# A residual tile held in SBUF, norm sums moved to TensorE, rstd by ln and exp, and a TensorE without waits on itself

## The chip, the cores and the metric

The kernel runs as one program on the eight NeuronCores of one Trainium2 chip, one batch element per core. The metric is the device time of the slowest core in microseconds (us). Cores 0 to 3 form die 0, cores 4 to 7 die 1. In some executions the cores of one die, or of both, are granted a lower TensorE clock and run some per cent longer (the changed kernel's own: 11180.00 us with mean clocks of 0.825 to 0.827 on die 1 and 0.877 on die 0, where its fast runs take 9956.56 to 9958.34 us at 0.950 to 0.959); such an execution is called slow here, whatever the kernel, and is never compared with a fast one. A second measure is used: the mean span of the four cores of an *undisturbed die*, meaning one whose mean granted clock was 0.95 or more, taken as the median over all such dies of a kernel's runs. Fast runs mostly have mean clocks of 0.95 to 0.96 on both dies.

## The reference

Two layers over 2048 latent tokens (and a 256-token context in front of the first mixer), each a macaron: SwiGLU feed-forward, token mixer, SwiGLU feed-forward. Layer 0 mixes with a bidirectional RG-LRU, layer 1 with a Fourier transform. Every sub-layer is wrapped in two RMS norms, so each reads and writes the residual stream `x`.

```python
def rmsnorm(x, g):
    y = x * lax.rsqrt(jnp.mean(x * x, axis=-1, keepdims=True) + EPS)
    return y * g

def ffn_sublayer(x, g_pre, g_post, shift, scale, gate, w_in, w_out):
    y = swiglu(modulate(rmsnorm(x, g_pre), shift, scale), w_in, w_out)
    return x + MACARON * gate * rmsnorm(y, g_post)

# one layer (D_MODEL 2048, D_FF 5632, fp32 in and out)
x = ffn_sublayer(x, g[0], g[1], sh1, sc1, gt1, ffn_w_in[i, 0], ffn_w_out[i, 0])
...                                              # context the same way, in layer 0
hx = modulate(rmsnorm(x, g[2]), sh2, sc2)
y = rglru_mixer(hx, hc, ...) if is_rec else fourier_mixer(hx, ...)
x = x + gt2 * rmsnorm(y, g[3])
x = ffn_sublayer(x, g[4], g[5], sh3, sc3, gt3, ffn_w_in[i, 1], ffn_w_out[i, 1])

# inside rglru_mixer, for each direction and for each of 16 channel groups
r = sigmoid(block_diag(v, wa, ba)); i = sigmoid(block_diag(v, wx, bx))
a = exp(-RG_C * r * softplus(-lam)); b = sqrt(-expm1(2 * log(a))) * i * v
h_t = a_t * h_{t-1} + b_t                        # linear scan
out = (gelu(g_lat) * (h_forward + h_backward)) @ w_out
```

## The kernel before

Operations are recorded with the tiles that they read and write, and waits are derived from that. Each engine counts its finished operations in a semaphore of its own (`E_pe`, `E_act`, ...). An operation that writes a tile waits for the tile's last writer, also where the last writer was the same engine:

```python
    def _wait(self, stream, ev):
        if ev is None:
            return
        key, val = ev
        if self.seen[stream].get(key, 0) >= val:
            return
        self.seen[stream][key] = val
        self.eng[stream].wait_ge(self.sems[key], val)
```

This reaches TensorE (PE) in the feed-forward output phases, where one PSUM pair (two sums of 128x512 fp32 side by side, `sbank(k, 0, n)` and `sbank(k, 1, n)`) is filled by two operations, one per half of the hidden width. The second waits until the first is finished, not just issued:

```python
            for (a, b) in parts:                 # [(0, 22), (22, 44)]
                ...                              # load this half's weights
                def pe(e, ...):
                    for h in range(2):
                        for c in range(a, b):
                            ins = e.matmul(sbank(k, h, n), buf[...], rhs(c, h), start=(c == 0), stop=(c == nk - 1))
                S.op("pe", pe, reads=[rb] + r_rhs, writes=spair_res(k))
```

The reciprocal root of a norm (`rstd`) takes ScalarE (ACT) and VectorE (DVE):

```python
        S.op("act", lambda e: e.activation(out=a3, in_=spair(k, n), func=AF.Sqrt, bias=epsb[:], scale=1.0 / D), ...)
        S.op("dve", lambda e: e.reciprocal(out=acc[:, :2 * n], in_=acc[:, :2 * n]), ...)
```

The RG-LRU loop issues, for each of 16 channel groups, the gates of this channel among the projection groups of the next one (`take`):

```python
            take(vch, 6)                         # six projection groups of the next channel
            for q in gq[0]:                      # gates, direction 0, each followed by one group
                q(); take(vch)
            pmul(c, 0)
            ...
            for q in gq[1]:
                q(); take(vch)
            pmul(c, 1)
            ...
            expo(c, 0); ...; expo(c, 1)          # exponentials, then the rest of the projections
            ...
            for d in range(2):
                msqrt(d); scan(d)
```

The *output map* `@ w_out` works on two tiles of 1024 tokens. Each of 16 steps makes one 128-row block of `y`, copies it to a ring buffer, stores it to HBM, squares it and adds the square to an accumulator on DVE. While tile 1 is computed, tile 0 is post-normed, added to `x` and pre-normed for its feed-forward, in half-blocks: `post_steps` loads `y` and `x` and stores `x`, and `pre_steps` loads `x` once more.

```python
        def mix_y(i, steps):
            acc, r_acc = accs[1 - i], r_accs[1 - i]
            it = Inter(steps, KC - 1)
            for m in range(KC):
                it.tick()                        # some post/pre steps of the other tile
                k = next_slot(); mix_mm(m, i, k, range(KC))        # (first three steps are cut here)
                load_wm(i * KC + m + 4)
                for h in range(2):
                    eb, re, dn = ev.next()       # ring of three buffers
                    S.op("act", ... func=AF.Copy ...)
                    S.dma("sp", dn + "y", ... out=ys[...], in_=eb[:] ...)
                    acc_add(acc, r_acc, 512, h, m == 0, sbank(k, h, 512), [rPS[2 * k + h]])
            it.flush()
        mix_y(0, None)
        mix_y(1, post_steps(tiles[0], 1, 0, 0, 1) + pre_steps(tiles[0], 0, 0, 2, W.dst, W.r_dst))
```

Of the kernel before, what the change touches and what calls it, by code (L numbers as in the profile page):

```python
# [8 lines left out]
F32 = mybir.dt.float32  # L9
BF16 = mybir.dt.bfloat16  # L10
AF = mybir.ActivationFunctionType
ALU = mybir.AluOpType
# [24 lines left out]
class Sched:  # L37
# [51 lines left out]
    def _wait(self, stream, ev):  # L89
        if ev is None:  # L90
            return
        key, val = ev
        if self.seen[stream].get(key, 0) >= val:
            return
        self.seen[stream][key] = val
        self.eng[stream].wait_ge(self.sems[key], val)
# [84 lines left out]
def build(nsub=6):  # L181
# [63 lines left out]
    def spair(k, n):  # L245
        return PS[:, k * 1024:(k + 1) * 1024].rearrange("p (h x) -> p h x", h=2)[:, :, :n]
# [47 lines left out]
    def modcol(l, q, kc, which):  # L294
        i = (q * 16 + kc) * 2 + which
        return mods[l][:, i:i + 1]
# [9 lines left out]
    def dercol(l, s, which, kind, kc):  # L306
        i = ((l * 3 + s) * 2 + which) * 32 + kind * 16 + kc
        return der[:, i:i + 1]
# [77 lines left out]
    def rstd(acc, r_acc, n, k=None, slot=None):  # L386
        if k is None:
            k = next_slot() if slot is None else slot

            def pe(e):  # L390
                ins = None
                for h in range(2):
                    ins = e.matmul(sbank(k, h, n), ones[:], acc[:, h * n:(h + 1) * n], start=True, stop=True)  # L393
                return ins
            S.op("pe", pe, reads=[r_acc, r_const], writes=spair_res(k))
        a3 = acc[:, :2 * n].rearrange("p (h x) -> p h x", h=2)
        S.op("act", lambda e: e.activation(out=a3, in_=spair(k, n), func=AF.Sqrt, bias=epsb[:], scale=1.0 / D),
             reads=spair_res(k) + [r_const], writes=[r_acc])
        S.op("dve", lambda e: e.reciprocal(out=acc[:, :2 * n], in_=acc[:, :2 * n]), reads=[r_acc], writes=[r_acc])

    def acc_add(acc, r_acc, n, h, first, src, r_src):
        a = acc[:, h * n:(h + 1) * n]
# [225 lines left out]
    def merged_segs(tl):  # L628
        out = []
        for h in range(2):  # L630
            for (off, w, src, dst, t0, which) in tl.halves[h]:
                off += h * tl.n
                p = out[-1] if out else None
                if p and p[0] + p[1] == off and p[2] is src and p[4] + p[1] == t0 and p[5] == which:
                    out[-1] = (p[0], p[1] + w) + p[2:]
                else:
                    out.append((off, w, src, dst, t0, which))
        return out

    def post_resident(tl, l, s, ro, xr, r_xr, yr, slot):  # L640
        n = tl.n
        segs = merged_segs(tl)
        acc, r_acc = accs[0], r_accs[0]
        q = []

        def load(m):
            yb, ry, dn = yr.next()
            S.dma("sp", dn, lambda e: e.dma_start(out=yb[:, :2 * n], in_=ys[tl.ysb, m, :, 0:2 * n]),
                  reads=r_ys[tl.ysb][m], writes=[ry])
            S.dma("sp", f"xr{m}", lambda e: [e.dma_start(out=xr[m][:, off:off + w], in_=src.ap[m, :, t0:t0 + w])  # L650
                                             for (off, w, src, dst, t0, which) in segs],
                  reads=[r for (off, w, src, dst, t0, which) in segs for r in src.r(m, t0, w)], writes=[r_xr[m]])
            q.append((yb, ry, ry.gen))
        for m in range(yr.n - 1):
            load(m)
        rstd(acc, r_acc, n, slot=slot)
        for m in range(KC):
            if m + yr.n - 1 < KC:
                load(m + yr.n - 1)
            yb, ry, gen = q.pop(0)  # L660
            assert ry.gen == gen
            x, rx = xr[m], r_xr[m]
            S.op("dve", lambda e: e.tensor_tensor(out=yb[:, :2 * n], in0=yb[:, :2 * n], in1=acc[:, :2 * n],
                                                  op=ALU.mult), reads=[r_acc], writes=[ry])
            for (off, w, src, dst, t0, which) in segs:
                S.op("dve", lambda e, off=off, w=w, which=which: e.scalar_tensor_tensor(
                    out=x[:, off:off + w], in0=yb[:, off:off + w], scalar=dercol(l, s, which, 1, m),
                    in1=x[:, off:off + w], op0=ALU.mult, op1=ALU.add), reads=[ry, r_der], writes=[rx])
            sv = yb[:].bitcast(BF16)[:, :2 * n]
            S.op("act", lambda e, sv=sv: e.activation(out=sv, in_=x[:, :2 * n], func=AF.Square), reads=[rx], writes=[ry])  # L670

            def stat(e, sv=sv, m=m):
                ins = None
                for h in range(2):
                    ins = e.matmul(sbank(slot, h, n), onesb[:], sv[:, h * n:(h + 1) * n], start=(m == 0), stop=(m == KC - 1))
                return ins
            S.op("pe", stat, reads=[ry, r_const], writes=spair_res(slot))
        for m in range(KC):
            S.dma("sp", f"xw{m}", lambda e, m=m: [e.dma_start(out=dst.ap[m, :, t0:t0 + w], in_=xr[m][:, off:off + w])
                                                  for (off, w, src, dst, t0, which) in segs],  # L680
                  reads=[r_xr[m]], writes=[r for (off, w, src, dst, t0, which) in segs for r in dst.r(m, t0, w)])
        rstd(rsx[ro], r_rsx[ro], n, slot)

    wi = Ring.at(sb_at, "wi", [W_MARK, W_MARK + 8192], [128, 16 * 256], BF16)
    wslots = {}
# [17 lines left out]
    def rglru(W0, tl, hx, hcb, r_hxs, tiles):  # L703
# [238 lines left out]
            proj(0, 0, b)  # L942
        for b in range(2):
            proj(0, 1, b)
        post_resident(tl, 0, 0, 1, xr, r_xr, yr, 3)
        segs = merged_segs(tl)
        n2 = 2 * tl.n
        for m in range(KC):
            tb, rt, _ = yr.next()
            S.op("dve", lambda e: e.tensor_tensor(out=tb[:, :n2], in0=xr[m][:, :n2], in1=rsx[1][:, :n2], op=ALU.mult),  # L950
                 reads=[r_rsx[1], r_xr[m]], writes=[rt])
            for (off, w, src, dst, t0, which) in segs:
                o = hcb[:, m, :] if which else hx[:, m, t0:t0 + w]
                rs = [r_hxs[m][16]] if which else r_hxs[m][t0 // 128:(t0 + w) // 128]
                S.op("act", lambda e, o=o, off=off, w=w, which=which: e.activation(  # L955
                    out=o, in_=tb[:, off:off + w], func=AF.Identity, bias=modcol(0, 3, m, which),
                    scale=dercol(0, 1, which, 0, m)), reads=[rt, r_der] + r_modq(0, 3), writes=rs)
        handover(r_xr + yr.res[:3], flat(r_gA) + flat(r_gB) + r_gM[0:1] + r_G[0] + wa.res[0:1])
        handover(yr.res[3:] + xl.res + ev.res + sq.res, r_vc[1] + r_gM[1:2] + wa.res[1:2])
        handover(r_accs + r_rsx, r_G[1] + [r_z])  # L960
# [42 lines left out]
        for c in range(KC):  # L1003
# [26 lines left out]
            gelu(c, 1)  # L1030
            if c > 0:
                hsum()
            take(vch, 6)
            for q in gq[0]:
                q()
                take(vch)
# [7 lines left out]
            for q in gq[1]:  # L1044
                q()
                take(vch)
            pmul(c, 1)
            if not last:
                ctx_proj(nx)
# [28 lines left out]
        r_accs.append(Res("acc1"))  # L1078
        after(r_accs[1:], pe_now())
        W = ffn_work(512, 5, HID0, HB0)  # L1080
        handover(gwr.res + r_vc[0] + r_vcb + flat(r_gA) + [wa.res[0], r_gM[0]] + flat(r_gB) + r_G[0], W.wr.res[2:])

        def mix_y(i, steps):
            acc, r_acc = accs[1 - i], r_accs[1 - i]
            it = Inter(steps, KC - 1)
            for m in range(KC):
                it.tick()
                if i == 0 and m < 3:
                    k = m
                    mix_mm(m, i, k, range(14, KC))  # L1090
                else:
                    k = next_slot()
                    mix_mm(m, i, k, range(KC))
                load_wm(i * KC + m + 4)
                for h in range(2):
                    eb, re, dn = ev.next()
                    S.op("act", lambda e, eb=eb, h=h, k=k: e.activation(out=eb[:], in_=sbank(k, h, 512), func=AF.Copy),
                         reads=[rPS[2 * k + h]], writes=[re])
                    S.dma("sp", dn + "y", lambda e, eb=eb, h=h, m=m: e.dma_start(
                        out=ys[tiles[i].ysb, m, :, h * 512:(h + 1) * 512], in_=eb[:]), reads=[re],  # L1100
                        writes=[r_ys[tiles[i].ysb][m][h]])
                    acc_add(acc, r_acc, 512, h, m == 0, sbank(k, h, 512), [rPS[2 * k + h]])
            it.flush()
        slot_i[0] = 3
        mix_y(0, None)
        after(W.r_hb_all(), pe_now())
        mix_y(1, post_steps(tiles[0], 1, 0, 0, 1) + pre_steps(tiles[0], 0, 0, 2, W.dst, W.r_dst))
        after(W.r_hid, pe_now())
        handover(wm.res, W.wr.res[0:2])
        W.wr.i = 2  # L1110
        accs.pop()
        r_accs.pop()
        return W, post_steps(tiles[1], 0, 1, 0, 1)

    def fold_w_steps():
        q = []
# [453 lines left out]
```

## Time and profile before

| | before |
|---|---|
| time, median of 3 runs | 10102.05 us (10095.14 to 10106.76) |
| span of the profiled core (core 4) | 10085.7 us |
| RG-LRU loop with the hand-over in front of it, core 4 | 839 us |
| output map, both tiles, core 4 (mean of eight cores) | 423 us (408) |
| seven feed-forward output phases, mean of eight cores | 2001 us |

The stage times are mine: from the first matmul of a stage to the first one of the next, found in the timeline by the tiles that the matmuls read. The output map's first tile is counted from the first matmul that reads its tile `zt`, which lies in the end of the last channel. "Seven output phases" are those of the nine that are followed directly by another feed-forward phase or by the loop; the other two run into the Fourier stage and into the end.

The first excerpt is the page of before: busy time of each engine with its share of the span, then for PE the busy tenths in 40 slices, PE's granted clock in tenths, and the queue that all `x` and `y` transfers use (packets, MB, share of the span of 16 DMA engines).

```profile
...
PE 8864.8 (88%) x47358; PEld 4321.4 (43%) x47995; DVE 2599.0 (26%) x3573; ACT 2004.9 (20%) x3036; POOL 615.1 (6%) x983
...
PE   2999899996887579999999999999965499999994
...
PEclk9999999998999789999999999999987799999997
...
q1 hardware_dynamic: 371584, 568.98, 20.0%
...
```

PE is busy nearly everywhere except at the start and the end, in slices 30 to 32 (around the Fourier stage) and in slices 10 to 15 (about 2270 to 3780 us): the hand-over, the RG-LRU loop and the output map. So most of the span is PE's, and only what PE does or waits for can shorten it.

The windows of the output map on core 4 (start and end, length, PE busy time, clock, DMA share, GB/s) and the list of PE's waits there (waiting instruction, what released it: total us, times, longest) show what PE lacks:

```profile
...
3235.00:3335.00 100.00, 93.69 (x421) 0.97 0.78 164
...
3435.00:3535.00 100.00, 30.17 (x127) 0.64 0.81 192
...
sum 400.00, PE 220.89; mean PE 55.22
```

```profile
...
PE PS L393 <- DVE rsx_17_71 L408: 74.3, 1, 74.3
PE PS L990 <- ACT sq_30_84 L407: 43.9, 3, 22.4
PE PS L393 <- DVE acc_16_70 L408: 35.1, 1, 35.1
...
```

In the first window, the first tile, PE is busy 94 of 100 us; in the third, within the second tile, 30. The second tile is a queue of norm statistics that wait for transfers through small rings: a PSUM pair is not free until its squares are taken, and the statistics of `x` cannot be summed until `x` has come. The DMA engines are at about 0.8 throughout. Each line of the list is one or a few long waits, not many short ones.

In the RG-LRU loop, ACT's waits on core 4 say that the tanh that opens a channel's gates waits for PE (13 times, up to 5.7 us):

```profile
...
ACT gA_45_21819 L853 <- PE PS L847: 73.7, 13, 5.7
...
```

Last, one reciprocal on DVE (start, us, instruction, shapes, idle before), and the rhythm of a feed-forward output phase on PE (44 matmuls per half, two halves per output block; starts are 9.49 and then 9.81 us apart, and the 0.32 us between the two are taken for the wait):

```profile
...
2394.22 4.95 DVE L399 RECIPROCAL acc_16_70<-acc_16_70 128x768 f32<-128x768 f32 x1 [16.37 <-ACT acc_16_70 L397]
...
```

```profile
...
4304.32 9.66 PE L598 MATMUL PS<-hid_29242,w_90_29240 128*128 128x512 bf16 x43
4313.81 9.66 PE L598 MATMUL PS<-hid_29242,w_91_29241 128*128 128x512 bf16 x43
4323.62 9.66 PE L598 MATMUL PS<-hid_29242,w_87_29237 128*128 128x512 bf16 x44
...
```

### The profile page before, as it was taken

Reading aid. Unit: us, or ns where it says so; the run is one execution under the profiler, and the core shown is the slowest. Engines: PE = TensorE matmul, PEld = TensorE weight load, DVE = VectorE, ACT = ScalarE, POOL = GpSimd, SP = SyncE. Lnnn points to the kernel's source line nnn. Section 1 sums busy time; section 2 is a strip of 40 time slices with the busy share of each in tenths; the row PEclk is TensorE's granted clock in tenths of the full one; section 3 lists DMA queues with packets and bytes.
Section 4 is the critical chain, followed back from the end, with each engine's and each line's share of the span. In section 5 each row is a group of like instructions: output and inputs, shape, how many; then the busy total and the mean of one; then the engine's idle time right before and its main releaser. Section 6 shows DMA issues by size and latency. Waiting matters only on the chain.

```text
span 10085.7 us, 126600 instructions; the slowest of 8 cores (10012.9 to 10085.7 us)
## 1 busy us (share of the span) xinstructions
PE 8864.8 (88%) x47358; PEld 4321.4 (43%) x47995; DVE 2599.0 (26%) x3573; ACT 2004.9 (20%) x3036; POOL 615.1 (6%) x983
## 2 busy tenths in 40 slices
PE   2999899996887579999999999999965499999994
PEld 1655555653333234444444444444423144444442
DVE  1112211224776422112211222122224322111102
ACT  1111111123675221111111101111113211110000
POOL 0000000000111000000000000000000000000000
PEclk9999999998999789999999999999987799999997
DMA  8779878886445877667766886677565677565545
GB/s 166 139 127 167 163 133 158 161 157 150 84 83 117 181 153 140 121 130 152 147 122 138 169 170 133 134 152 151 117 155 154 168 142 138 112 131 123 118 89 138
DMA packets 524533, 1407.96 MB, mean 140 GB/s; under 512 B 64408, under 2 KB 194584, under 8 KB 470944
## 3 DMA queue, kind: packets, MB, share of 16 engines
q0 software_dynamic: 152352, 830.83, 48.9%
q1 hardware_dynamic: 371584, 568.98, 20.0%
q8 instruction: 398, 6.52, 0.3%
q14 instruction: 199, 1.63, 0.1%
HBM read 1987.87 MB, written 221.25 MB: 219 GB/s over the span
## 4 chain that ended last, share of the span: by engine, by line
PE 77%; DMA 13%; DVE 3%; ACT 3%; issue 3%; SPq 1%; DVEq 0%; ACTq 0%; POOL 0%; POOLq 0%
PE PS L178 45%; PE PS L598 25%; PE PS L781 3%; DMA wfs<-ev_28_82 2%; DMA wfs<-ev_26_80 1%; DMA w_36_90<-modw 1%; PE PS L866 1%; DMA wfs<-ev_27_81 1%; PE PS L990 1%; DMA xl_25_79<-xs 1%; PE PS L349 1%; DMA xl_22_76<-xs 1%; DMA xl_21_75<-xT 1%; PE PS L393 1%; DMA xl_24_78<-xs 1%
## 5 line engine op out<-in xcount | busy, mean ns | idle before, releaser
L408 DVE TENSOR_TENSOR acc_16_70<-acc_16_70,sq_29_83 128x512 f32<-128x512 f32 (+1 forms) x150 | 97.8, 652 | 2055.0 <-ACT sq_29_83 L407 2025.6
L178 PE MATMUL PS<-hb_29243,w_90_29240 128*128 128x512 bf16 x2381 | 531.9, 382 | 13.0 <-DVE mods_3_45 L356 8.8
L178 PE MATMUL PS<-hb_29243,w_89_29239 128*128 128x512 bf16 x2315 | 513.6, 380 | 14.2 <-ACT ev_26_80 L571 10.5
L178 PE MATMUL PS<-hb_29243,w_88_29238 128*128 128x512 bf16 x2128 | 477.9, 383 | 33.9 <-DVE mods_3_45 L356 21.6
L178 PE MATMUL PS<-hb_29243,w_87_29237 128*128 128x512 bf16 x2127 | 470.5, 379 | 3.9 <-ACT ev_28_82 L571 0.6
L178 PE MATMUL PS<-hb_29243,w_91_29241 128*128 128x512 bf16 x2069 | 458.0, 379 | 3.8 <-DVE mods_3_45 L356 1.3
L178 PE MATMUL PS<-hb_92,w_35_89 128*128 128x384 bf16 x2176 | 364.9, 329 | 11.8 <-DVE mods_2_44 L356 11.5
L178 PE MATMUL PS<-hb_92,w_34_88 128*128 128x384 bf16 x2048 | 340.4, 327 | 35.3 <-ACT hb_92 L474 35.3
L178 PEld LDWEIGHTS PS<-hb_29243,w_90_29240 128*128 128x128 bf16 x2432 | 238.3, 98 | 298.5 <-issue 18.3
L178 PE MATMUL PS<-hb_92,w_36_90 128*128 128x384 bf16 x2176 | 361.1, 327 | 2.9 <-DVE mods_2_44 L356 2.7
L178 PEld LDWEIGHTS PS<-hb_29243,w_89_29239 128*128 128x128 bf16 x2368 | 230.8, 98 | 288.4 <-issue 13.6
L178 PE MATMUL PS<-hb_92,w_33_87 128*128 128x384 bf16 x2048 | 338.0, 326 | 0.0
L178 PEld LDWEIGHTS PS<-hb_29243,w_88_29238 128*128 128x128 bf16 x2176 | 213.2, 99 | 290.5 <-issue 41.6
L571 ACT ACTIVATE ev_28_82<-PS 128x512 f32<-128x512 f32 (+1 forms) x266 | 148.7, 559 | 881.5 <-PE PS L178 787.3
L178 PEld LDWEIGHTS PS<-hb_29243,w_87_29237 128*128 128x128 bf16 x2176 | 211.7, 98 | 254.7 <-issue 1.3
L178 PEld LDWEIGHTS PS<-hb_29243,w_91_29241 128*128 128x128 bf16 x2112 | 205.8, 98 | 248.8 <-issue 2.2
L571 ACT ACTIVATE ev_27_81<-PS 128x512 f32<-128x512 f32 (+1 forms) x264 | 147.6, 559 | 817.6 <-PE PS L178 777.7
L571 ACT ACTIVATE ev_26_80<-PS 128x512 f32<-128x512 f32 (+1 forms) x262 | 146.1, 558 | 817.2 <-PE PS L178 769.7
L781 PE MATMUL PS<-hx_19516,wi_31_85 128*128 128x512 bf16 x992 | 250.3, 380 | 45.2 <-ACT hcb_19517 L955 26.6
L178 PEld LDWEIGHTS PS<-hb_92,w_35_89 128*128 128x128 bf16 x2176 | 214.1, 99 | 156.8 <-issue 19.5
L178 PEld LDWEIGHTS PS<-hb_92,w_36_90 128*128 128x128 bf16 x2176 | 213.1, 98 | 144.4 <-issue 5.1
L178 PEld LDWEIGHTS PS<-hb_92,w_34_88 128*128 128x128 bf16 x2048 | 200.5, 98 | 168.6 <-issue 38.2
(700 smaller groups left out, 12459.1 us busy)
## 6 DMA issues: line engine op xcount, KB each, us to landing
w_90_29240<-win POOLq DMA_DIRECT2D x38, 1024.0 KB, 10.2
w_89_29239<-win POOLq DMA_DIRECT2D x37, 1024.0 KB, 11.4
w_35_89<-win POOLq DMA_DIRECT2D x34, 1024.0 KB, 10.2
w_36_90<-win POOLq DMA_DIRECT2D x34, 1024.0 KB, 9.7
w_87_29237<-win POOLq DMA_DIRECT2D x34, 1024.0 KB, 11.5
w_88_29238<-win POOLq DMA_DIRECT2D x34, 1024.0 KB, 11.7
w_91_29241<-win POOLq DMA_DIRECT2D x33, 1024.0 KB, 10.4
w_34_88<-win POOLq DMA_DIRECT2D x32, 1024.0 KB, 10.6
```

The source lines that it names most:

```text
L178: ins = e.matmul(out, l, r, start=(i == 0), stop=(i == n - 1))
L349: ins = e.matmul(o, w, scb[:, 2 * c:2 * c + 2], start=(c == 0), stop=(c == KC - 1))
L393: ins = e.matmul(sbank(k, h, n), ones[:], acc[:, h * n:(h + 1) * n], start=True, stop=True)
L408: S.op("dve", lambda e: e.tensor_tensor(out=a, in0=a, in1=sb[:, :n], op=ALU.add), reads=[rsq], writes=[r_acc])
L571: S.op("act", lambda e, tb=tb, h=h, k=ks[0]: e.activation(out=tb[:, :n], in_=sbank(k, h, n), func=AF.Silu), reads=[rPS[2 * ks[0] + h]], wr ...
L598: ins = e.matmul(sbank(k, h, n), buf[:, (c - a) * 128:(c - a + 1) * 128], rhs(c, h), start=(c == 0), stop=(c == nk - 1))
L781: ins = e.matmul(sbank(k, b % 2, 512), buf[:, kk * 256 + o:kk * 256 + o + 128], hx[:, kk, b * 512:(b + 1) * 512], start=(kk == 0), stop=(k ...
L866: ins = e.matmul(PS[:, 3072 + h * 512:3584 + h * 512], wg(d, g), vcb[:, lo + h * 512:lo + (h + 1) * 512], start=True, stop=True)
L990: ins = e.matmul(sbank(k, h, 512), buf[:, c * 128:(c + 1) * 128], zt[i][:, c, h * 512:(h + 1) * 512], start=(c == 0), stop=(c == KC - 1))
```

## The change

Four things are changed together. (1) PE never waits for its own semaphore; this takes for granted that its operations finish in order. (2) rstd is `exp(-0.5 ln(.))` on ACT alone. (3) In the RG-LRU loop two projection groups move from ahead of direction 0's gates to behind direction 1's. (4) In the output map the residual tile is loaded once into SBUF, updated there, used for the next pre-norm there and stored once; its norm sums, and those of `y`, are matmuls with ones on PE, where before they were additions on DVE.

```diff
-        if self.seen[stream].get(key, 0) >= val:
+        if self.seen[stream].get(key, 0) >= val or (stream == "pe" and key == "E_pe"):
             return
...
-        S.op("act", ... func=AF.Sqrt, bias=epsb[:], scale=1.0 / D), ...
+        S.op("act", ... func=AF.Ln, bias=epsb[:], scale=1.0 / D), ...
-        S.op("dve", lambda e: e.reciprocal(...
+        S.op("act", lambda e: e.activation(out=acc[:, :2 * n], in_=acc[:, :2 * n], func=AF.Exp, scale=-0.5), ...
...
-            take(vch, 6)
+            take(vch, 4)
             for q in gq[0]: ...
             for q in gq[1]: ...
+            take(vch, 2)
             pmul(c, 1)
...
-    def post_resident(tl, l, s, ro, xr, r_xr, yr, slot):      # same work, in the hand-over before the loop
+    class Resident:                     # load_x, load_y, post (update x, square, stat), store, pre
...
+                if PE statistics of the previous step are pending: issue them here
                 for h in range(2):      # copy and store y as before, without acc_add
+                S.op("act", ... out=sv, in_=PS[:, k * 1024:(k + 1) * 1024], func=AF.Square ...)
+                pend.append(... two matmuls with ones ...)
+                for st in sched.get(m, []):
+                    st()
...
+        for m in range(KC):
+            R.load_x(m)                 # 16 loads, 8.4 MB, on SyncE's queue
+        mix_y(0, 3, {})
+        begin()                         # y loads, rstd of y
+        sched = {m + 1: [lambda m=m, i=i: R.post(2 * m + i, kp[0]) for i in range(2)] for m in range(8)}
+        sched[9] = [middle]             # rstd of x
+        for m in range(KC):             # pre and store, in steps 10 to 15
+            sched.setdefault(10 + m * 6 // KC, []).append(lambda m=m: pre2(m))
+        mix_y(1, ky, sched)
```

Lines with `...` are cut, and two `+` lines (the members of `Resident`, the pending statistics) tell in words what is longer in the kernel.

## The prediction

> **What bounds the kernel now.** TensorE: the page shows PE busy 88% of 10085.7 us, the windows 49-50 us of every 50 in the feed-forwards. Elsewhere it waits: in the RG-LRU channel loop (42 of 50 us), at the RG-LRU output map (windows 3235-3635 us: PE 221 of 400), in the Fourier mixer and the tail.
>
> **Output map.** Its first tile runs without gaps (92 of 98 us). The second takes 302 us for 129 us of PE work at DMA share 0.82: the list of waits shows PE stuck 74.3, 35.1 and 62.5 us behind statistics that wait, through small rings, for transfers (chain of waits: `xl<-xs` 5-28 us each). With x held in SBUF, one of four activation transfers of 8.4 MB goes; by the page's queue shares (569 MB in 20.0% of the span) one costs some 30 us of all DMA engines (estimate). Costs:
> - 96 more matmuls (21 us) for norm sums.
> - All 16 x loads are issued just ahead of the first y stores, on the same queue. [...] With three eviction buffers I expect ScalarE, then PE, to stall about 30 us [...]: first tile 101 -> 131 us.
> - In eight steps of the second tile PE waits in order for two squares behind the evictions, about 4.7 us each (copies 0.48, squares 1.1): 12 us per step, not 6.9. Then steps of 7.4-9 us while x is stored. Second tile 298 -> 180 us.
> Net -85 us (-40 to -125).
>
> **PE without waits on itself.** Program order shows the second half of each feed-forward output group waiting for its first. The timeline shows 9.81 us for such a half against 9.49: 0.31 us x 9 phases x 16 = 44 us, nearly all critical: -43. In the RG-LRU loop four-matmul groups start 1.17 us apart, not 0.87. A channel takes 46.3 us. PE alone would save 5, but the path exponentials, root, multiply (2.56), scan (4.96), next tanh becomes the limit, and two projection groups moved behind the gates delay it by 1.5: -2.9 us per channel, -42 in all.
>
> **rstd.** VectorE's reciprocal takes 6.55 us (1024 columns) or 4.95 (768); exp should take 1.1 or 0.9. [...] the coefficient's exp and ln sharing one load (1.28 us). Of 26 some six are critical (start, two before the RG-LRU loop, two before the Fourier stage, end): -27.
>
> **Total.** -43 -42 -27 -85 = -197: **9905 us, range 9855 to 9965**. Chances: faster by over 2% 0.44, within 2% 0.55, slower 0.01.
>
> **What would show it.**
> - Output map 400 -> 315 us; a 20-40 us stall just after its start, ScalarE waiting for a y store; 4-6 us PE gaps in the second tile's first half.
> - Feed-forward output groups without the 0.31 us gap; each phase 5 us shorter.
> - Channel period 43.4 us, first tanh waiting for VectorE's scan, no longer PE.
> - No reciprocal; one table load per rstd.
>
> **What would make it wrong.** The y stores passing the x loads, or squares running ahead, would give 30 us more each; so would a loop that follows PE rather than the scan. Stores of x colliding with weights, or a second table load per rstd, give less; a cold clock after each gap some 15 us less.

That the first `y` store would wait for the `x` loads ahead of it was my expectation; no trace then showed it. The stall of 30 us is an estimate from the page of before: 569 MB in 20.0% of 10085.7 us is 282 GB/s, at which 8.4 MB take 30 us. The times of the new exp, also an estimate, are those of the Sqrt in the same place, 1.11 us for 1024 columns and 0.90 for 768. The exp and ln of the coefficient share a load at 2375.04 us on core 4: 1.28 us at L747, none at L749. The cold clock was seen in before: on core 4, after 21.05 us in which PE waited, 31 matmuls took 9.84 us instead of 7.07, with PEclk at 0.50 from 3374.4 to 3398.2 us. The 15 us for it, 1.9 us for each of eight steps, are an estimate; those 2.77 us for 31 matmuls are what before shows.

## The result, and the profile after

The changed kernel took 9957.88 us, median of 4 runs, one of them slow (9956.56 to 11180.00), against 10098.59 us for before, also 4 runs. The ratio of the fast runs is 0.9862, 95% interval 0.9843 to 0.9881: within 2%, 141 us less, where 197 were predicted. A ratio is the mean time of one kernel's fast runs over that of the other's of the same rounds, so it is not quite the ratio of these medians. The time lies inside the predicted range (9855 to 9965), near its upper end. The outputs are right.

| stage, mean of eight cores of the profiled execution | before | after | |
|---|---|---|---|
| seven short feed-forward output phases | 2001 | 1971 (die 0: 1963, die 1: 1980) | -29 |
| two long ones, into the Fourier stage and to the end | 892 | 877 | -16 |
| gate and up phases | 5213 | 5212 | -1 |
| RG-LRU loop with hand-over | 840 | 796 | -44 |
| output map | 408 | 377 | -31 |
| Fourier stage | 492 | 487 | -5 |
| mean span | 10045 | 9919 | -127 |

Differences are taken before rounding. The eight cores gain 127 us on average and the slowest 129 (10085.7 to 9957.0).

The mean hides a difference between the dies: die 0 gains 153 us and die 1, which sets the time, 100. The clock records in the trace show why in part. In this execution the cores of die 1 were granted 0.81 of the clock in 76 to 90 bursts of at most 11.3 us, 377 to 480 us in all (the window from 2543.9 to 2552.7 us on core 4 is one, at a PEclk of 0.81); die 0 had none, nor had any core in the profiled execution of before. If PE was busy throughout, the bursts cost 71 to 90 us (an estimate: the records say 0.8125, so 0.1875 of their length). In the other two fast executions die 1 has the same mean clock, 0.950 to 0.954. What brings the bursts on is open: on the chip of group a below they also occur on die 1 in a3_rstd (764 to 1075 us, mean clock 0.938 to 0.944 there and 0.955 to 0.957 on die 0), which keeps all waits, and on the other two chips the fast profiles of b1, b2, c0 and c1, which drop the waits, have none (mean clocks of 0.956 to 0.963 on all cores).

The page of after:

```profile
...
PE 8893.2 (89%) x47440; PEld 4372.1 (44%) x48079; DVE 2410.6 (24%) x3408; ACT 2016.8 (20%) x2999; POOL 614.1 (6%) x983
...
q1 hardware_dynamic: 364672, 560.58, 19.1%
...
```

VectorE lost 188 us of work (2599.0 to 2410.6), and 8.4 MB of `x` are gone from the queue (568.98 to 560.58). The output map, core 4, the sum over four windows of 100 us and PE's waits:

```profile
...
sum 400.00, PE 286.01; mean PE 71.50
```

```profile
...
PE PS L1132 <- ACT sq_30_84 L1126: 73.3, 4, 35.3
PE PS L682 <- ACT ym_110_28323 L676: 7.8, 4, 4.0
...
```

PE is busy 286 of 400 us (was 221), but two single waits of 33 to 35 us stand out. The timeline places them. PE waits for a square, and in each case ACT had itself waited for a store of `y` to leave its eviction buffer (first fence PE, second ACT):

```profile
...
3225.32 1.01 PE L1132 MATMUL PS<-sq_30_84,onesb_48 128*128 128x512 bf16 x2 [35.31 <-ACT sq_30_84 L1126]
...
3542.65 1.01 PE L1132 MATMUL PS<-sq_30_84,onesb_48 128*128 128x512 bf16 x2 [33.05 <-ACT sq_30_84 L1126]
...
```

```profile
...
3223.66 0.60 ACT L1119 ACTIVATE ev_26_80<-PS 128x512 f32<-128x512 f32 x1 [34.76 <-DMA ys<-ev_26_80]
...
3541.00 0.60 ACT L1119 ACTIVATE ev_26_80<-PS 128x512 f32<-128x512 f32 x1 [27.20 <-DMA ys<-ev_26_80]
...
```

The first is the stall that was predicted, 16 loads of `x` ahead of the first `y` store. The second, at the end of the second tile, was not in the sum. Between them lie eight steps such as this one on PE:

```profile
...
3363.28 0.59 PE L682 MATMUL PS<-ym_112_28325,onesb_48 128*128 128x512 bf16 x2 [2.86 <-ACT ym_112_28325 L676]
3364.44 0.63 PE L682 MATMUL PS<-ym_113_28326,onesb_48 128*128 128x512 bf16 x1 [0.57 <-ACT ym_113_28326 L676]
3364.87 8.54 PE L1013 MATMUL PS<-zt_81_22236,wm_85_22240 128*128 128x512 bf16 x32
3373.25 0.59 PE L1132 MATMUL PS<-sq_29_83,onesb_48 128*128 128x512 bf16 x2
3376.71 0.59 PE L682 MATMUL PS<-ym_114_28327,onesb_48 128*128 128x512 bf16 x2 [2.86 <-ACT ym_114_28327 L676]
...
```

The step from 3363.28 to 3376.71 takes 13.43 us: two gaps of 2.86 and 0.57 us in front of the two `x` statistics (L682), and 32 matmuls in 8.54 us, in the next step 31 in 8.76, where 32 matmuls at a PEclk of 1.00 take 7.07 (b3_defer below shows them at that, and so does the step at 3418.36 us on this core). In the loop the first tanh now waits for VectorE's scan, and the moved projection groups show as waits of the convolution that follows them (`vcA`; a1 below, without the move, has no such wait and a2, with it, has):

```profile
...
ACT gA_45_21454 L870 <- DVE gM_49_21458 L917: 36.4, 14, 3.2
...
ACT vcA_21452 L810 <- PE PS L798: 10.3, 7, 1.5
...
```

The output phases lost the pause (steps 9.49 to 9.50 us where before had 9.49, 9.81), and rstd is one table load with two activations on ACT:

```profile
...
4229.48 9.66 PE L598 MATMUL PS<-hid_28305,w_91_28304 128*128 128x512 bf16 x43
4238.98 9.66 PE L598 MATMUL PS<-hid_28305,w_87_28300 128*128 128x512 bf16 x44
...
```

```profile
...
3326.85 1.28 ACT L397 ACT_TABLE_LOAD   x1 [0.82 <-PE PS L1132]
3328.14 1.11 ACT L397 ACTIVATE acc_86_28299<-PS,epsb_50 128x1024 f32<-128x1024 f32 x1
3329.35 1.06 ACT L399 ACTIVATE acc_86_28299<-acc_86_28299 128x1024 f32<-128x1024 f32 x1
```

### The profile page after: what moved, and what is told of

It reads as the page before. It is cut to its first block, busy times and chain, and to the rows that moved or that the text cites. A ratio compares the mean times of both kernels' runs of the same rounds, so it can differ in the third digit from the quotient of the medians.

```text
span 9957.0 us, 124360 instructions; the slowest of 8 cores (9864.1 to 9957.0 us)
## 1 busy us (share of the span) xinstructions
PE 8893.2 (89%) x47440; PEld 4372.1 (44%) x48079; DVE 2410.6 (24%) x3408; ACT 2016.8 (20%) x2999; POOL 614.1 (6%) x983
## 3 DMA queue, kind: packets, MB, share of 16 engines
q1 hardware_dynamic: 364672, 560.58, 19.1%
## 4 chain that ended last, share of the span: by engine, by line
PE 79%; DMA 10%; ACT 3%; DVE 3%; issue 2%; SPq 1%; DVEq 0%; ACTq 0%; POOL 0%; POOLq 0%
PE PS L178 48%; PE PS L598 25%; PE PS L1013 2%; PE PS L798 1%; DMA w_36_90<-modw 1%; PE PS L883 1%; DVE gM_49_21458 L917 1%; DMA wfs<-ev_26_80 1%; PE PS L349 1%; SPq L647 1%; DMA wfs<-ev_27_81 0%; DMA ys<-ev_26_80 0%; DMA xl_21_75<-ys 0%; PE PS L393 0%; DVE gB_47_21456 L914 0%
## 5 line engine op out<-in xcount | busy, mean ns | idle before, releaser
L178 PE MATMUL PS<-hb_28306,w_90_28303 128*128 128x512 bf16 x2381 | 536.2, 384 | 4.8 <-ACT acc_16_70 L397 1.8
L178 PE MATMUL PS<-hb_28306,w_89_28302 128*128 128x512 bf16 x2315 | 521.6, 384 | 3.8 <-issue 0.5
L178 PE MATMUL PS<-hb_28306,w_88_28301 128*128 128x512 bf16 x2128 | 475.7, 382 | 15.1 <-DVE mods_3_45 L356 11.8
L178 PE MATMUL PS<-hb_28306,w_87_28300 128*128 128x512 bf16 x2127 | 476.9, 383 | 3.4 <-issue 0.5
L178 PE MATMUL PS<-hb_28306,w_91_28304 128*128 128x512 bf16 x2069 | 462.6, 382 | 2.5
L598 PE MATMUL PS<-hid_28305,w_90_28303 128*128 128x512 bf16 x1164 | 263.9, 384 | 5.2 <-DVE hid_28305 L573 1.9
```

Source lines behind the costliest of these rows:

```text
L178: ins = e.matmul(out, l, r, start=(i == 0), stop=(i == n - 1))
L598: ins = e.matmul(sbank(k, h, n), buf[:, (c - a) * 128:(c - a + 1) * 128], rhs(c, h), start=(c == 0), stop=(c == nk - 1))
```

## The experiments

Eleven kernels were run, in three groups: the four named a on one chip, b0, b1, b3 and b4 on a second, b2, c0 and c1 on a third, each with runs of before on the same chip between them. The table uses undisturbed dies (number of them in brackets); before differs by 28 us between the second chip and the third, which limits comparisons across groups to about that.

| kernel | mean span, us | before, same chip | difference |
|---|---|---|---|
| before, no PE self-wait (a1_nowait) | 9935 (4) | 10047 (5) | -112 |
| the same and the groups moved (a2_nowait_move) | 9967 (5) | 10047 | -80 |
| before with ln and exp (a3_rstd) | 10032 (4) | 10047 | -15 |
| changed kernel with the old output map (a4_old_map) | 9958 (7) | 10047 | -89 |
| changed kernel, control (b0_after) | 9910 (7) | 10027 (13) | -117 |
| `y` stores of tile 0 on ACT's queue (b1_actq) | 9889 (8) | 10027 | -138 |
| `x` statistics one step later (b3_defer) | 9870 (6) | 10027 | -157 |
| `x` stored early (b4_store) | 9887 (8) | 10027 | -140 |
| `x` loads spread (b2_spread) | 9901 (9) | 10055 (8) | -154 |
| groups not moved (c0_nomove) | 9892 (10) | 10055 | -163 |
| b2, b3, b4 and c0 together (c1_all) | 9819 (9) | 10055 | -236 |

The theory was this. The self-wait, the loop and rstd give what the prediction said; the output map gives about half, because the new transfers and the new order on PE make three new waits: at the start, in eight steps, and at the end. The rival: the map gives its 85 us, and the rest is lost elsewhere, to a lower clock or to the loop.

### 1. The parts without the map (a1_nowait, a2_nowait_move, a3_rstd)

a1_nowait is before with this alone; a2_nowait_move adds the move; a3_rstd is before with the new rstd alone.

```diff
-        if self.seen[stream].get(key, 0) >= val:
+        if self.seen[stream].get(key, 0) >= val or (stream == "pe" and key == "E_pe"):
             return
```
```diff
-            take(vch, 6)
+            take(vch, 4)
...
                 take(vch)
+            take(vch, 2)
             pmul(c, 1)
```
```diff
-        S.op("act", ... func=AF.Sqrt, bias=epsb[:], scale=1.0 / D), ...
-        S.op("dve", lambda e: e.reciprocal(...
+        S.op("act", ... func=AF.Ln, bias=epsb[:], scale=1.0 / D), ...
+        S.op("act", ... func=AF.Exp, scale=-0.5), ...
```

Expected of a1_nowait:

> The kernel before with one part of the change: TensorE does not wait on its own semaphore. My theory: each of the nine feed-forward output phases gets 5 us shorter (0.31 us for each of 16 groups), and in the RG-LRU loop the path expo, root, multiply, scan, next tanh takes over as the limit. As the two projection groups are not moved here, that path is 1.5 us shorter per channel than in the changed kernel, so the channel takes 46.3 - 4.4 = 41.9 us and the loop gains about 65 us. In all -90 to -110 us. Rival A: the loop follows PE, and the moved groups are what the gain of the loop (45 us in the changed kernel) comes from; then this kernel gains 40 in the phases and under 30 in the loop, -70 us. Rival B: a denser PE is granted a lower clock, which eats the gain of the phases: then the granted clock in the output phases is under that of before by over 1%, and the nine phases together gain under 25 us on the die where it happens.

Expected of a2_nowait_move:

> As a1, and the two projection groups moved behind the gates, as the change has it. My theory: the move delays the convolution's ScalarE pass, and so the exponentials and the scan, by 1.5 us per channel; 15 to 25 us slower than a1, -75 to -90 us against before. Rival A: the move helps (it lets the gates start earlier): 10 us or more faster than a1.

Expected of a3_rstd:

> The kernel before with rstd by ln and exp alone. My theory: some six of 26 rstds lie on the critical path, 4 to 5.5 us each, so -20 to -30 us; 26 reciprocals (136 us of VectorE time) gone and one table load per rstd as before. Rival: VectorE's reciprocals also held up the hidden products at the start of the gate and up phases, so more than -40 us; or the loads double and it is under -10.

Measured: a1 -112 us, just beyond the far end of what the theory gave (-110) and well off its rival A; a2 -80, inside its range, but 32 us slower than a1 where 15 to 25 were expected; a3 -15, below its range. The loop (mean of die 0; 841 us in before) took 780 in a1, 808 in a2 and 831 in a3. So dropping the waits alone gives 61 us in the loop, and moving the groups gives 28 of them back. PE's waits for ACT's gate activations in the loop, core 1, without the move and then with it:

```profile
...
PE PS L866 <- ACT gB L853: 14.9, 26, 0.9
...
```

```profile
...
PE PS L866 <- ACT gB L853: 46.7, 26, 3.1
...
```

The moved groups stand on PE between the gates and ACT's exponentials, and the exponentials head the path to the scan and to the next channel's tanh. The list fits that, but the verdict rests on the stage times: the prediction charged the move with 1.5 us per channel, it measures (808 - 780)/16 = 1.75. By stages rstd gave 10 us in the loop and some 9 in the output phases, the map and the Fourier stage together (means of die 0); the gate and up phases, which it does not touch, were 10 us longer in that execution.

The runs of a1 had a slow die 1 throughout. In the profiled execution die 0 was slow too: cores 0 and 1 from 8235 us on, cores 2 and 3 from about 165 to 2043 us (mean clocks 0.922 to 0.926 on the four). The loop lies between and had no such stretch on these cores; on core 1 it ran at a clock of 0.93 as in before. Nothing is concluded from a1's medians. Rival B of a1, a clock lowered by the denser PE (a guess that no trace had shown), did not show in the four executions with an undisturbed die 0 (clock 0.955, as in before); on die 1 of that chip the clock was low with and without the change, so it is not tested there.

### 2. The changed kernel with the old output map (a4_old_map)

```diff
-        (the new mix_y, Resident tile, begin, middle, sched)
+        (mix_y, post_steps and pre_steps of before)
```

> The changed kernel with the output map of before (tile not resident, sums on VectorE there); all else as changed. My theory: without self-waits and with rstd by exp it is at -95 to -115 us against before, and so 30 to 45 us behind the changed kernel (-140): the resident map is worth only about 40 us, as the traces of before and after say (423 to 383 us for both tiles). Rival: the residency is worth the 85 us that I predicted and the other parts less than thought; then this kernel is at -60 us or less gain.

Measured: -89 us, a little less than expected, and close to a2 and a3 added (-95): the parts other than the map add up. The map took 402 us on die 0, where the changed kernel took 375, with the old long wait back in PE's list (core 1):

```profile
...
PE PS L393 <- DVE rsx L408: 73.1, 1, 73.1
...
```

So the new map is worth 402 - 375 = 27 us by its stage, and by the spans 117 - 89 = 28 across two chips. The rival is out as far as the map goes: it does not give its 85 us, they are missing in the map itself. No run separates the two halves of the new map, the tile kept in SBUF and the norm sums on PE.

### 3. The start of the first tile (b0_after, b1_actq, b2_spread)

The control is the changed kernel itself. b1_actq sends the first tile's `y` stores by ACT's own queue; b2_spread issues one `x` load per step, behind that step's `y` stores.

```diff
-                    S.dma("sp", dn + "y", lambda e, eb=eb, h=h, m=m: e.dma_start(
+                    S.dma("act" if i == 0 else "sp", dn + "y" + str(i), lambda e, eb=eb, h=h, m=m: e.dma_start(
```
```diff
-        for m in range(KC):
-            R.load_x(m)
-        mix_y(0, 3, {})
+        mix_y(0, 3, {m: [lambda m=m: R.load_x(m)] for m in range(KC)})
```

Expected of the control:

> The changed kernel again, as the control for the three runs that follow it on the same chip. Every theory expects what was measured before: 135 to 145 us under the kernel before (ratio about 0.986) in fast runs; mean span of the cores of an undisturbed die 0 about 9903 us against about 10045; in the output map one wait of PE of some 35 us at the start of the first tile, eight steps of about 13.4 us and one wait of PE of 25 to 35 us at the end of the second. If the slow state rules again, die 0 at a clock of 0.95 or more is compared.

Expected of b1_actq:

> The changed kernel, but the y stores of the output map's first tile are issued by ScalarE's own queue instead of SyncE's, where the sixteen x loads are ahead of them. Theory (order in the ring: the first y store waits its turn behind 8.4 MB of x): the start wait of 35 us shrinks to under 8 us, the first tile falls from 166 to 130 to 140 us, the kernel is 25 to 35 us faster than the control. Rival (the DMA engines are simply full while x is loaded, whatever the queue): the start wait stays at 20 us or more and the time within 10 us of the control.

Expected of b2_spread:

> The changed kernel, but the sixteen x loads are issued one per step of the output map's first tile, each behind that step's y stores, instead of all ahead of the first. Theory (order in the ring): PE's wait of 32 to 36 us at the start of the first tile falls under 5 us, no other wait grows by more than 5 us, the output map (first and second tile together, 373 us on an undisturbed core of die 0) falls to 335 to 345 us, the time of an undisturbed die 0 to 9870 to 9885 us where the changed kernel had 9903 to 9914. Rival (x's 8.4 MB cost the same wherever they lie): the wait comes back as waits for y stores or for weights in later steps and the map stays above 360 us.

The control behaved as expected in the map (373 us on cores 0 and 1, waits of 36.3 us at the start and 33.9 at the end) with a smaller gain than in the first measurement, 117 us, and only one fast run, 9945.62 us. The same wait at the start in the three kernels, core 1, in the order control, b1, b2:

```profile
...
3222.59 1.01 PE L1132 MATMUL PS<-sq,onesb 128*128 128x512 bf16 x2 [36.32 <-ACT sq L1126]
...
```

```profile
...
3183.94 0.59 PE L1132 MATMUL PS<-sq,onesb 128*128 128x512 bf16 x2 [2.98 <-ACT sq L1126]
...
3194.60 1.01 PE L1132 MATMUL PS<-sq,onesb 128*128 128x512 bf16 x2 [8.83 <-ACT sq L1126]
...
3235.77 0.75 PE L1132 MATMUL PS<-sq,onesb 128*128 128x512 bf16 x2 [2.40 <-ACT sq L1126]
...
```

```profile
...
3198.24 0.59 PE L1132 MATMUL PS<-sq,onesb 128*128 128x512 bf16 x2 [1.77 <-ACT sq L1126]
...
3205.90 1.01 PE L1132 MATMUL PS<-sq,onesb 128*128 128x512 bf16 x2 [6.20 <-ACT sq L1126]
...
```

With the stores on another queue 36 us become 14 (2.98, 8.83 and 2.40), with the loads behind the stores they become 8. The map takes 358 us in b1 and 349 in b2, means of eight cores, against 377. So the order of issue on the queue was most of the stall: 36.32 us with 16 loads ahead of the first `y` store, 8 with each load behind a step's stores. b1 keeps 14 us while its stores run beside 8.4 MB of loads (the DMA share in the 50 us after 3200 is 0.98); what its stores wait for there is not shown. Both expectations of no remaining wait above 5 or 8 us failed by a few us. By spans b1 is 21 us under the control where 25 to 35 were expected, and b2's die 0 stood at 9902 us, not at 9870 to 9885. For b2 the spans say only 9 us against the control on another chip, but 37 (154 - 117) by the differences to before; I rely on the stage.

### 4. The eight steps (b3_defer)

```diff
-            S.op("pe", stat, reads=[ry, r_const], writes=spair_res(slot))
+            if self.late is None:
+                ...                              # as before
+            else:
+                self.late.append(lambda: (S.op("pe", stat, ...), self.load_y()))
...
                 while pend:
                     pend.pop(0)()
+                while R.late:                    # one step later, behind that step's matmuls
+                    R.late.pop(0)()
```

One more `y` load is issued at the beginning, since each next one now follows the late statistic.

> The changed kernel, but in the second tile the two norm-sum matmuls of each x tile are put one step later in PE's order, so that PE doesn't wait for ScalarE's squares of the same step. Theory (PE waits in order for two squares behind two evictions): the gaps of 2.9 and 0.4 us in each of the eight steps vanish, PE's clock recovers, a step falls from 13.4 to 9 to 10.5 us, the second tile loses 20 to 35 us and the kernel as much, unless the x stores behind it then come sooner. Rival (the steps are bound by the y and weight transfers or by VectorE, with DMA share near 0.8): the steps stay at 12 us or more, the gap only changes its name, gain under 10 us.

Measured: 40 us under the control, the most of the single edits and a little over what was expected. PE's timeline on core 1 has no gap left in these steps:

```profile
...
3357.10 1.03 PE L681 MATMUL PS<-ym,onesb 128*128 128x512 bf16 x4
3357.96 7.07 PE L1016 MATMUL PS<-zt,wm 128*128 128x512 bf16 x32
...
3365.30 1.03 PE L681 MATMUL PS<-ym,onesb 128*128 128x512 bf16 x4
...
```

A step takes 3365.30 - 3357.10 = 8.20 us; 9 to 10.5 were expected. It loses the gaps (3.2 us) and also up to 1.7 us in each 32 matmuls, which are back at 7.07 us. The map falls from 375 to 336 us (die 0), and 8 x (3.2 + 1.7) = 39. The lower clock shows in the records: on core 4 of the changed kernel's first profile PEclk is 0.50 for 3.41 us in seven of the eight steps (the first from 3350.77 us), which costs 3.41 / 2 = 1.7 us of matmuls (an estimate). The control on core 1 has the same pattern, 32 matmuls in 8.10 to 8.76 us in seven steps and in 7.07 in one, and a PEclk over windows of 50 us of 0.89 to 0.91 there; in b3 it is 1.00. The wait at the end of the tile is still there (31.1 us at 3496.32).

### 5. The end of the second tile (b4_store)

```diff
             R.pre(m, 0, 0, 2, pdst2)
-            R.store(m)
-        sched = {m + 1: [lambda m=m, i=i: R.post(2 * m + i, kp[0]) for i in range(2)] for m in range(8)}
+        sched = {m + 1: [lambda m=m, i=i: (R.post(2 * m + i, kp[0]), R.store(2 * m + i)) for i in range(2)] for m in range(8)}
```

> The changed kernel, but each x tile is stored as soon as its update is done (steps 1 to 8 of the second tile) instead of bunched in steps 10 to 15. Theory (the bunched 8.4 MB of x stores hold up the last y stores and meet the weight prefetch): the wait of 27 us of ScalarE for a y store and PE's of 33 us at the end of the second tile vanish, the second tile falls from 217 to 180 to 195 us, the kernel is 20 to 35 us faster than the control. Rival (x's bytes cost the same DMA time wherever they lie): steps 1 to 8 grow from 13.4 to 16 us or more and the kernel is within 10 us of the control.

Measured: 23 us under the control, the map 345 us against 377. The last steps on PE, core 1:

```profile
...
3500.08 0.59 PE L1132 MATMUL PS<-sq,onesb 128*128 128x512 bf16 x2
3505.34 1.01 PE L1132 MATMUL PS<-sq,onesb 128*128 128x512 bf16 x2 [4.67 <-ACT sq L1126]
...
```

Of 33.9 us at the end 4.7 remain, and the eight steps are not longer than they were (13.3 to 13.4 us between the waits at 3373.74, 3387.16 and 3400.59), though the DMA share in them rises from 0.58 to 0.93. The stores of `x` cost no PE time where DMA time lay idle, and some 30 us where they meet the weights of the next phase. On core 4 of the changed kernel, from 3500 to 3530 us, the weights' queue took most of the DMA engines' time, and the `y` stores had the stores of `x` ahead of them on their own (packets, MB, share of the 16 engines; q0 is the weights' queue, q1 SyncE's):

```profile
...
q0 software_dynamic: 788, 4.54, 89.2%
q1 hardware_dynamic: 667, 1.23, 12.1%
...
```

b4 takes the stores of `x` away from both, so how the wait divides between the order in the queue and the meeting with the weights is not shown.

### 6. Without the move, and all together (c0_nomove, c1_all)

c0_nomove is the changed kernel with `take(vch, 6)` ahead of the gates again. c1_all has the edits of b2, b3 and b4 and this one.

```diff
-            take(vch, 4)
+            take(vch, 6)
...
-            take(vch, 2)
             pmul(c, 1)
```

Expected of c0_nomove:

> The changed kernel, but the two projection groups of the RG-LRU loop stay ahead of the gates, as in the kernel before. Theory (the moved groups lie on the path exponentials, root, multiply, scan, next tanh): the loop loses 1.5 us per channel, 795 to 800 us become 770 to 780, the kernel is 20 to 32 us faster than the changed one (9880 us or so for an undisturbed die 0), as between the two runs of the kernel before with and without the move. Rival (with the new rstd and the eight slots of a channel the move fills PE's gap and pays): no change, or slower by up to 10 us.

Expected of c1_all:

> The changed kernel with four edits together: x loads spread over the first tile, each x tile stored after its update, the second tile's norm-sum matmuls one step later, and the projection groups back ahead of the gates. If the four act apart, the output map goes from 373 to 265 to 285 us (PE alone needs 264), the loop from 798 to 775, and an undisturbed die 0 from 9909 to about 9780 us: 250 to 270 us under the kernel before, ratio 0.973 to 0.976. If x's traffic is what bounds the map, 8.4 MB in and 8.4 MB out at the 200 to 250 GB/s that the traces show beside weights and y, the map stays above 310 us and die 0 above 9820.

c0: the loop falls from 796 to 773 us (mean of eight cores), the map stays at 375. By spans it is 18 us under the control and 46 by the differences to before, so the stage's 23 is the number to trust.

c1: fast runs of 9830.10 to 9853.76 us, ratio to before 0.9752 (95% interval 0.9721 to 0.9783). That is 2.5% under before, though the record's verdict is "unclear" (three fast runs against two), and about 1.1% under the changed kernel, whose ratio was 0.9862 on another chip. Undisturbed dies are at 9819 us, not the 9780 expected. The loop is at 773, the map at 299, against 377 in the changed kernel and savings of 28, 39 and 32 with b2, b3 and b4: 78 us saved where the three added promise 99. PE's longest remaining waits in the map are eight for squares, 27 us:

```profile
...
PE PS L1136 <- ACT sq L1130: 27.2, 8, 6.9
...
```

```profile
...
3200.00:3250.00 50.00, 50.00 (x233) 1.00 0.93 219
...
3300.00:3350.00 50.00, 41.57 (x177) 0.93 1.02 261
...
```

The DMA share is now 0.90 to 1.02 from 3200 us on. That suggests that the transfers themselves now begin to limit the map; no run tests it. Neither theory's number for c1 (265 to 285, or above 310) was right; 299 lies between. About 20 of the 40 missing us are in the map; where the others are is open, the long output phases (880 us) and the gate and up phases (5216) vary by that much from core to core and run to run.

## Why the prediction was right, and where its terms were off

The class (within 2%, the likelier of the two it named) and the range held. That the range held with the largest term failing owes something to its width: it reached 60 us above its middle, and the time used 53 of them. Point by point:

- **PE without waits on itself: -43 in the output phases.** Right. The seven short phases lose 37 us on die 0, 5.3 us each, and 38 on all eight cores in the fast run of b1 (1963 us against 2001). In the first profile die 1 lost only 22. The phases in which its core 4 stays behind core 0 are those with a lower clock (0.96 and 0.98 in the third and the sixth, where core 0 has 0.97 and 1.00), so part of this gain was hidden on the very cores that set the time.
- **The loop: -42.** Close: a2 shows 841 to 808, -33, limit and delay as described (the first tanh waits for the scan; the move costs 1.75 us per channel, charged at 1.5). What the prediction did not draw from its own 1.5 us is that leaving the move out would pay: a1 shows -61 without it.
- **rstd: -27.** Mis-sized. The mechanism held (one load of 1.28 us, then 1.11 and 1.06 us, no reciprocal), but a3 gained 15 us, of which 10 in the loop. So not all of the six rstds counted as critical hold something up; which ones do not was not taken apart, except that the two before the loop do.
- **The output map: -85.** This is the term that failed, and it fell outside its own range of -40 to -125: -31 as a mean of eight cores, -40 on the profiled core 4 (first tile +42 where +30 was said, second -82 where -118 was said), -27 by a4. Three things:
  - It was read from the slowest core, whose map took 423 us; the mean is 408. 15 us of its 423 were that core's own.
  - The second tile's steps were put at 12 us and take 13.4: the gaps were smaller than thought (3.2 us, not 4.7) but the 32 matmuls after them take 8.2 to 8.8 us in seven of the eight steps on core 4, instead of 7.07. The prediction listed a cold clock after each gap as a risk of 15 us; b3 shows 14 of its 40 us to be that (8 x 1.7, at a clock of 0.50 for 3.41 us).
  - The last steps were put at 7.4 to 9 us "while x is stored". They hold a wait of 33 us instead. It was named among the risks ("stores of x colliding with weights") and not costed; b4 shows that it is worth 32 us in the stage.
- **Start stall of 30 us: 34.8 us** on ACT in core 4. Right in cause and size, shown by b1 and b2.

Together: 54 us are missing in the map, 12 in rstd, 9 in the loop, and the output phases of an undisturbed die gave some 6 more than predicted (nine of 5.4 us, an estimate from the seven). That makes 69. The shortfall is 56 by the fast runs (197 - 141), 70 by the mean span of the profiled execution (197 - 127) and 44 on its die 0 (197 - 153). The sum agrees no better than that, and before itself moves by 28 us between chips.

## What to carry to other kernels

Taking a transfer away helped here only as far as the remaining ones were issued at the right time: with 8.4 MB less the map had three new waits (35 us, eight steps with 26 us together, 33 us), and each of them went, or fell to 8 us and under, with a change of a few lines in the order of issue (spread bulk loads behind the small urgent stores, store bulk data where the DMA share is low, put a dependent matmul one step later in PE's order). A gap of 3.2 us on PE cost up to half as much again (1.7 us, with PEclk at 0.50 for 3.41 us) in the matmuls after it. When two edits are bundled, run them apart: here the move of two projection groups gave back 28 of the 61 us that dropping the waits had won.

## What the traces show of the hardware

- Every ACT table load in these records takes 1.28 us. In the rstd above the load starts at 3326.85, the ln at 3328.14 us, as the load ends, and the exp at 3329.35 without a load of its own (none of the 27 on core 4 has one), so this rstd by ln and exp costs 1.28 + 1.11 + 1.06 us.
- Two gaps of PE, of 2.86 us (4.00 in the first step) and 0.35 to 0.57 us, were followed by a PEclk of 0.50 for 3.41 us in seven of the eight steps on core 4 of the changed kernel, and the next 32 matmuls took 8.2 to 8.8 us instead of 7.07. In the sixth step the gaps are 3.08 and 0.35 us, the clock stays at 1.00 and the matmuls take 7.07. What decides between the two is not shown.
- All eight cores held a granted clock of 0.99 to 1.00 through most gate and up phases of fast runs (1.00 from 1200 to 1500 us on all eight, in before and in after). A clock of 0.81 does occur: for long stretches in slow executions, and in fast ones on single dies: in bursts of at most 11.3 us on die 1 in the changed kernel's (480 us in all on core 4), and for some 160 us on cores 6 and 7 in b4's (mean clocks 0.955 and 0.953, the other six 0.958 to 0.960). What grants it no run shows. The same 100 us of the span on core 1, first in the control's slow execution, then in the changed kernel's fast one:

```profile
...
4300.00:4400.00 100.00, 100.00 (x383) 0.81 0.51 106
...
```

```profile
...
4300.00:4400.00 100.00, 100.00 (x465) 1.00 0.63 128
...
```

- One VectorE instruction with two SBUF inputs took longer where it overlapped a GpSimd addition (POOL L922). Its 128x2304 take 2.56 us on core 4 in before and 5.64 us in after, where it starts 1.28 us into GpSimd's 4.50 us; 4.50 - 1.28 + 2.56 = 5.78, as if it had made no progress until GpSimd was done. Of 32 such instructions on core 4 in after, the 15 that start within that addition take 3.96 to 5.66 us, all within 0.15 us of that sum, and the other 17 take 2.55 to 2.56 us. In the profile this is a longer VectorE instruction, not idle time. No run shows that it cost the kernel time.

```profile
...
2727.26 2.56 DVE L880 SCALAR_TENSOR_TENSOR gB_47_21821<-gB_47_21821,vcB_21828 128x2304 f32<-128x2304 f32 x1 [4.69 <-ACT gB_47_21821 L870]
...
```

```profile
...
2742.94 4.50 POOL L922 TENSOR_TENSOR gM_50_21459<-gM_50_21459,gM_49_21458 128x2048 f32<-128x2048 f32 x1 [11.02 <-DVE gM_50_21459 L917]
...
2744.22 5.64 DVE L897 SCALAR_TENSOR_TENSOR gB_47_21456<-gB_47_21456,vcA_21452 128x2304 f32<-128x2304 f32 x1 [1.43 <-ACT gB_47_21456 L887]
...
```

- A 256 KB store issued behind 8.4 MB of loads on one queue waited 35 us (ACT's wait for it is 34.76 us on core 4), 14 us of waits remained on another issuing engine's queue, and 8 us with the loads issued behind it.
